# A skip product made one stage earlier, and a normaliser that reads its columns in place: an mLSTM recurrence on one core

## The chip, the cores and the metric

The kernel runs on one core of a Trainium2 chip as one program with one launch. The metric is the device time of that launch in microseconds. The kernel before took 2337.57 us (median of three executions, 2334.41 to 2339.46). One more execution was recorded by the hardware profiler; every duration below comes from that one.

A core has TensorE (PE in the profile, its weight loads PEld), VectorE (DVE), ScalarE (ACT), GpSimd (POOL) and SyncE (SP). Each takes its instructions in a fixed order; SP here issues nearly all DMA transfers. PSUM is the memory that TensorE writes to.

## The reference, cut to what matters

Two layers over 1024 latent and 256 context tokens of width 1024. Layer 0 is an attention layer, which the change doesn't touch. Layer 1 is a bidirectional mLSTM with 8 heads of 256 channels (2048 channels in all):

```
xm, z, og = split(h @ w_in, 3)                     # 2048 channels each
xc  = silu(conv5(xm))                              # over tokens
q, k, v = blockdiag(xc), blockdiag(xc), blockdiag(xm)
# per direction, per head, over chunks of tokens:
num = sqk @ v + inter * (C @ q)                    # C: the 256 x 256 state before the chunk
den = rowsum(sqk) + inter * (n . q)
h  += num / max(|den|, exp(-m))                    # both directions are added
# output
hn  = rmsnorm_per_head(sigmoid(og) * h) * head_norm
y   = ((hn + skip * xc) * silu(z)) @ w_out
```

Two places matter here. The first is `skip * xc`: a product of the convolved features, which are known before the recurrence starts, with one number per channel. The second is `max(|den|, exp(-m))`: the normaliser, for which `exp(-m)` has been worked out for all tokens, heads and directions before the recurrence.

## The kernel before, in words

All arithmetic is in 32 bits. Most matrix products are made from operands split into a high and a low part (`Ops.split`: `hi` on lines 59 to 63, `lo` on line 67) and three matmuls (`mm3`, lines 78 to 80). Layer 1 has these stages:

- **Features** (`phase_a`). A loop over 16 blocks of 128 channels. For each block TensorE projects the 1280 tokens (tile `xps`, three PSUM buffers), ScalarE copies the result to `xp` (line 962), the convolution runs on ScalarE and VectorE (lines 983 and 985), ScalarE makes `xc = silu(...)` (line 986), and SP stores `xc` to the DRAM tensor `xcT` (lines 987 and 988). Then come the gate sums (line 995), `v` (lines 1008 to 1010), `q` (tile `qt`, lines 1017 and 1018) and the gate branch `z` (two halves, line 942, stored by line 1024). The tile of `q` and the tile of `z` are two allocations of one tag, `qt`, in the pool `qp`, which has two buffers of 128x1024.
- **Gates** (`gate_scan`, inside `phase_z`). The running sums and maxima of the gates, which end in the tiles `gcol0` and `gcol1`, one for each direction: for each chunk of 128 tokens and each head four columns, of which column 1 is `exp(-m)`.
- **Recurrence** (`phase_b`). 32 units, each a head `h` and a block `c` of 256 tokens. A unit has five parts: `states` (the state updates of the next head; it loads `x` from `xcT` by line 1225 and `v` by line 1227, and transposes `x` on TensorE), `front` (multiplies `q` by `x` on TensorE, line 1257, and makes the decay factors `E`), `mid` (the numerators and denominators, tile `num` of 128 x 4 x 258, whose column 256 is the denominator), `combine` (the normaliser, the output gate, the norm) and `back` (transposes the result, adds the skip product, multiplies by `silu(z)`, stores `u`). In the code of one unit they stand in the order `mid`, `states`, `front` of the next unit, `combine`, `back` of the unit before.
- **Output projection** (`out1`).

Where the change is made: in `combine`, line 1304 copies the two columns of `exp(-m)` of each direction into a small tile `e` on POOL (two copies of 128x2), lines 1306 and 1307 make `max(|den|, e)` on VectorE and line 1308 its reciprocal, which scales `num` on ScalarE (line 1311) and VectorE (line 1312). In `back`, line 1333 multiplies the tile `x` in place by the skip factor on ScalarE (two instructions of 128x256), line 1334 adds the transposed result on VectorE, line 1335 multiplies by `sz` on POOL, and line 1338 stores `u` from the same tile. So a tile `x` is held from `states` until its store has landed, with 8 buffers.

Within these stages the instruction order of each engine's queue and of SP's is made by a planner when the program is built: it simulates the program with its own durations and takes what is ready first. (Only `phase_z` fixes an order by hand, for TensorE and ScalarE.) A changed instruction can thus shift the order around it. Buffers of a tag are handed out by the same planner.

Of the kernel before, what the change touches and what calls it, by code (L numbers as in the profile page):

```python
# [11 lines left out]
F32 = mybir.dt.float32  # L12
F32R = mybir.dt.float32r
AF = mybir.ActivationFunctionType
ALU = mybir.AluOpType
# [4 lines left out]
P = 128  # L20
D = 1024
KT = D // P
SEQ, CTX = 1024, 256
T = SEQ + CTX
NT = T // P
# [8 lines left out]
F = 2 * D  # L34
NF = F // P
MH = 8
LAT_COLS = 258
# [4 lines left out]
U = 256  # L42
# [870 lines left out]
def phase_a(nc, tc, ops, A, consts, mod, hT, S, W, graw, wx0, late):  # L913
# [3 lines left out]
    with ExitStack() as es:  # L917
        pl = lambda name, bufs=1, **kw: es.enter_context(tc.tile_pool(name=name, bufs=bufs, reuse_waits="tile", **kw))
        cp, wp, sp, qp = pl("a_c"), pl("a_w", 2), pl("a_s", 2), pl("a_q", 2)
# [2 lines left out]
        nc.sync.dma_start(wif, A["w_if"])  # L922
        cw = cp.tile([P, NF, 6], F32, name="cw")
        nc.sync.dma_start(cw, A["conv"])
        gw = [cp.tile([P, 2, P], F32R, name=f"gw{i}") for i in range(2)]
        xps = [cp.tile([P, CONV_W + 4], F32, name=f"xp{i}") for i in range(2)]
        for i in range(2):
# [3 lines left out]
        cols = [(0, 256), (LAT_COLS, 512), (LAT_COLS + 512, 512)]  # L931
# [12 lines left out]
        for f in range(NF):  # L944
# [6 lines left out]
            xp = xps[f % 2]  # L951
# [30 lines left out]
            xc = sp.tile([P, CONV_W], F32, name="xc")  # L982
# [3 lines left out]
            nc.scalar.activation(xc, xc, AF.Silu)  # L986
            nc.sync.dma_start(S["xcT"][f, :, :CTX], xc[:, :CTX])
            nc.sync.dma_start(S["xcT"][f, :, CTX:], xc[:, LAT_COLS:])
            xh = [sp.tile([P, CONV_W], F32R, name=f"xc{i}", bufs=1) for i in "hl"]
            ops.split(xh[0], xh[1], xc, "pool", "dve")  # L990

# [20 lines left out]
            qt = qp.tile([P, SEQ], F32, name="qt")  # L1012
# [62 lines left out]
def gate_scan(nc, tc, ops, A, consts, S, keep, raw, es):  # L1075
# [2 lines left out]

    cols = [keep.tile([P, NT, 4, MH], F32, name=f"gcol{d}") for d in range(2)]
    dec = keep.tile([P, 2, MH, NCH], F32, name="decay")
    pl = lambda name, bufs=1, **kw: es.enter_context(tc.tile_pool(name=name, bufs=bufs, reuse_waits="tile", **kw))
    sp, pp = pl("g_s"), pl("g_p", 1, space=PSUM)
# [17 lines left out]
    e = new("ge")  # L1102
# [48 lines left out]
    for c0 in range(0, NT, 3):  # L1151
        n = min(3, NT - c0)
# [5 lines left out]
        for d, r in enumerate(rows):  # L1158
            nc.vector.tensor_copy(cols[d][:, c0 : c0 + n], pt[:, :n, :, r.start : r.start + MH])
    nc.sync.dma_start(dec, S["dec"].rearrange("d h c -> (d h c)").unsqueeze(0).partition_broadcast(P))  # L1160
    yield cols, dec


def phase_b(nc, tc, ops, A, consts, S, W, cols, dec, hT, es_h, es_w):

    with ExitStack() as es, ExitStack() as ew, ExitStack() as eo:
        pl = lambda name, bufs=1, st=es, **kw: st.enter_context(
            tc.tile_pool(name=name, bufs=bufs, reuse_waits="tile", **kw)  # L1170
# [2 lines left out]
        cp, lp, rp, vp, xp = pl("b_c"), pl("b_l", 2), pl("b_r", 2), pl("b_v"), pl("b_x")  # L1173
# [3 lines left out]
        hns = cp.tile([P, 2, NF], F32, name="hns")  # L1177
# [11 lines left out]
        def update(h, d, i, st):  # L1189

            t, nxt = ORDERS[d][i : i + 2]
            c, a = divmod(t, 2)
            acol = cols[d][:, t, 2, h : h + 1]
            ah = [sp.tile([P, VW], F32R, name=f"ah{i}", bufs=AHB) for i in "hl"]
            va = st["v"][c][:, a]
            nc.scalar.activation(ah[0], va, AF.Copy, scale=acol)  # L1196
            nc.vector.scalar_tensor_tensor(ah[1], va, acol, ah[0].bitcast(F32), ALU.mult, ALU.subtract)  # L1197
            pk = [pc.tile([P, 512], F32, name="pc")[:, :VW] for k in range(2)]
            for k in range(2):
                ops.mm3(pk[k], [x[:, a, k * P : (k + 1) * P] for x in st["th"][c]], ah, True, True)  # L1200
            new = st["C", d, nxt] = state()
            old = st.get(("C", d, t))
            if old is None:
                for k in range(2):
                    nc.scalar.copy(new[0][:, k], pk[k])  # L1205
            else:
                decay(h, d, t, st, pk)
# [12 lines left out]
        def states(h, step, st):  # L1220

            for c in news[step]:
                hd = slice(h * 256, (h + 1) * 256)
                x = st["x"][c] = xp.tile([P, 2, U], F32, name="x", bufs=8)
                nc.sync.dma_start(x, S["xcT"][2 * h : 2 * h + 2, :, c * U : (c + 1) * U].rearrange("k p t -> p k t"))
                v = st["v"][c] = vp.tile([P, 2, VW], F32, name="v", bufs=7)
                nc.sync.dma_start(v[:, :, :256], S["v"][c * U : (c + 1) * U, hd].rearrange("(a p) d -> p a d", p=P))
                nc.gpsimd.memset(v[:, :, 256:257], 1.0)
                nc.gpsimd.memset(v[:, :, 257:258], 0.0)
                pt = pw.tile([P, 2, 2, P], F32, name="S")  # L1230
                for a in range(2):
                    for k in range(2):
                        nc.tensor.transpose(pt[:, a, k], x[:, k, a * P : (a + 1) * P], consts["idn"])
                th = st["th"][c] = [sp.tile([P, 2, 256], F32R, name=f"th{i}", bufs=THB) for i in "hl"]
                ops.split(th[0], th[1], pt.rearrange("p a k f -> p a (k f)"), "act", "dve")
            for i in (2 * step, 2 * step + 1):
                for d in range(2):
                    update(h, d, i, st)

            for d in range(2):  # L1240
                if step == 1:
                    update(h, d, NCH - 2, st)
                if step == 3:
                    t, nxt = ORDERS[d][-2:]
                    decay(h, d, t, st, st["C", d, nxt][0])
# [49 lines left out]
        def combine(h, c, st):  # L1295

            og = lp.tile([P, 2, 256], F32, name="og")
            tok = slice((c - 1) * U, c * U)
            nc.sync.dma_start(og, S["og"][tok, h * 256 : (h + 1) * 256].rearrange("(c p) d -> p c d", p=P))
            ms = rp.tile([P, 2], F32, name="ms")  # L1300
            r, e = (rp.tile([P, 2, 2], F32, name=x) for x in ("r", "e"))
            num = st["n", c]
            for d in range(2):
                nc.gpsimd.tensor_copy(e[:, d], cols[d][:, 2 * c : 2 * c + 2, 1, h])
            den = num[:, :, 256].rearrange("p (d a) -> p d a", d=2)
            nc.vector.scalar_tensor_tensor(r, den, -1.0, den, ALU.mult, ALU.max)
            nc.vector.tensor_tensor(r, r, e, ALU.max)
            nc.vector.reciprocal(r, r)
            for a in range(2):
                n0, n1 = (num[:, 2 * d + a, :256] for d in range(2))  # L1310
                nc.scalar.activation(n0, n0, AF.Copy, scale=r[:, 0, a : a + 1])
                nc.vector.scalar_tensor_tensor(n0, n1, r[:, 1, a : a + 1], n0, ALU.mult, ALU.add)
                nc.gpsimd.tensor_tensor(n0, n0, og[:, a], ALU.mult)  # L1313
                nc.scalar.activation(n1, n0, AF.Square, scale=1.0 / 16, accum_out=ms[:, a : a + 1])
            ops.rsqrt(ms, ms)
            for a in range(2):
                n0 = num[:, a, :256]
                nc.scalar.activation(n0, n0, AF.Copy, scale=ms[:, a : a + 1])

        def back(h, c, st):  # L1320

            tok = slice((c - 1) * U, c * U)
            x = st["x"][c]
            sz = xp.tile([P, 2, U], F32, name="sz", bufs=2)
            nc.sync.dma_start(sz, S["sz"][2 * h : 2 * h + 2, :, tok].rearrange("k p t -> p k t"))
            pt = pw.tile([P, 2, U], F32, name="S")
            for k in range(2):
                for a in range(2):
                    n0 = st["n", c][:, a]
                    nc.tensor.transpose(pt[:, k, a * P : (a + 1) * P], n0[:, k * P : (k + 1) * P], consts["idn"])  # L1330
            for k in range(2):
                f = 2 * h + k
                nc.scalar.activation(x[:, k], x[:, k], AF.Copy, scale=hns[:, 1, f : f + 1])
                nc.vector.scalar_tensor_tensor(x[:, k], pt[:, k], hns[:, 0, f : f + 1], x[:, k], ALU.mult, ALU.add)
            nc.gpsimd.tensor_tensor(x, x, sz, ALU.mult)  # L1335

            q = nc.gpsimd if (h, c) == units[-1][:2] else nc.sync
            q.dma_start(S["u"][2 * h : 2 * h + 2, :, tok].rearrange("k p t -> p k t"), x)
# [17 lines left out]
        for step in range(NU - 1):  # L1356
            states(0, step, sts[0])
            gate(0, ogt[step], o)
        units = [(h, c, sts[h]) for h in range(MH) for c in range(1, NU)]
        front(*units[0])  # L1360
        for i, (h, c, st) in enumerate(units):
# [12 lines left out]
            if nxt:  # L1374
                states(h + 1, c - 1, sts[h + 1])
                n = len(ogt)
# [121 lines left out]
def build(nc, tc, A, out, dbg=None):  # L1498
    ops = Ops(nc)
    with ExitStack() as es:  # L1500
        cp = es.enter_context(tc.tile_pool(name="const", bufs=1))
# [17 lines left out]
        def ahead(oT_d):  # L1519
# [3 lines left out]
        oT_d = layer0(nc, tc, ops, A, consts, mod, dp, ahead, dbg)  # L1523
        W = o0.W
        shapes = {
            "xcT": [NF, P, T], "qT": [NF, P, SEQ], "v": [T, F], "sz": [NF, P, SEQ], "og": [SEQ, F],
            "u": [NF, P, SEQ], "dec": [2, MH, NCH], "negM": [2, MH, T],
        }
        S = {n: dp.tile(s, F32, name=n + "_d") for n, s in shapes.items()}
        gk = es.enter_context(tc.tile_pool(name="gk", bufs=1))  # L1530
        with ExitStack() as el:
# [20 lines left out]
            with ExitStack() as e1:  # L1552
                scan = gate_scan(nc, tc, ops, A, consts, S, gk, graw, e1)
                next(scan)
                cols, dec = phase_z(nc, tc, ops, A, hT, S, W, range(NZ), scan)
        ew = es.enter_context(ExitStack())
        begun = phase_b(nc, tc, ops, A, consts, S, W, cols, dec, hT, eh, ew)
        out1(nc, tc, ops, A, mod, S, x1d, out, *begun)
        if dbg:
# [102 lines left out]
```

## Time and profile before

The profiled execution took 2338.38 us, of which 2336.6 us are the span from its first to its last instruction.

| engine | busy us | share of the span |
|---|---|---|
| PE | 2233.6 | 96% |
| PEld | 1957.4 | 84% |
| DVE | 1583.1 | 68% |
| ACT | 1185.5 | 51% |
| POOL | 1140.5 | 49% |

The features run from about 1050 to 1570 us of the span, the gates and the first states to about 1700 us, the 32 units of the recurrence from about 1700 to 2156 us, and the output projection takes the rest. The shares above are averages over stages with different limits. A busy time of PE includes time in which a matmul passes through the engine's pipeline, so a PE shown as busy needn't be at its peak. A line such as `ACT num L1311 <- DVE r L1308: 41.5, 24, 4.1` says that ScalarE's instruction of line 1311 waited for VectorE's of line 1308, 41.5 us in total, 24 times, at most 4.1 us. Lines 59 to 85 are helpers, which many tiles share.

### The profile page before, as it was taken

How to read it: one execution, taken by the hardware profiler on the slowest of the kernel's cores; microseconds unless marked ns; L12 is line 12 of the kernel's file. 1: busy time of each engine (PE TensorE's matmuls, PEld its weight loads, DVE VectorE, ACT ScalarE, POOL GpSimd, SP SyncE). 2: the span in 40 equal slices, each digit the busy share in tenths (PEclk: the TensorE clock that was granted, in tenths of full speed). 3: DMA queues.
4: the chain of work that ended last, by engine and by line, in shares of the span. 5: the costliest groups of instructions: out<-in, count | busy, mean ns of one | idle time of the engine just before them, and what ended most of it. 6: DMA issues, size and time to landing. Idle time of an engine off the chain costs nothing. (4 is left out here: it accounts for less than half of the span.)

```text
span 2336.6 us, 38014 instructions
## 1 busy us (share of the span) xinstructions
PE 2233.6 (96%) x13488; PEld 1957.4 (84%) x13488; DVE 1583.1 (68%) x2753; ACT 1185.5 (51%) x2864; POOL 1140.5 (49%) x1572
## 2 busy tenths in 40 slices
PE   8998999999999999998999999998999999998998
PEld 4877898998998988887878888878988888897787
DVE  5589489999998988467454443345188888898321
ACT  3512488787887877332322222233267666676211
POOL 3424356565655645462222111136557888788321
PEclk9999999999999999999999999999999999999999
DMA  7066522222311211543444333332645555545531
GB/s 262 28 197 228 160 71 79 64 68 67 89 45 58 82 54 53 191 160 123 143 131 130 120 115 109 119 122 94 193 129 164 164 168 167 163 140 169 183 126 54
DMA packets 189273, 291.10 MB, mean 125 GB/s; under 512 B 14136, under 2 KB 134712, under 8 KB 188828
## 3 DMA queue, kind: packets, MB, share of 16 engines
q1 hardware_dynamic: 188556, 286.84, 38.7%
q8 instruction: 107, 1.75, 0.3%
q0 software_dynamic: 528, 1.84, 0.2%
q14 instruction: 82, 0.67, 0.1%
HBM read 198.00 MB, written 90.62 MB: 124 GB/s over the span
## 5 line engine op out<-in xcount | busy, mean ns | idle before, releaser
L688 POOL TENSOR_SCALAR P<-P,sc 128x512 f32<-128x512 f32 (+1 forms) x384 | 243.5, 653 | 138.8 <-ACT P L644 64.8
L67 DVE TENSOR_TENSOR PTl<-tps,PTh 128x512 fp32r<-128x512 f32 x336 | 228.8, 683 | 13.5 <-ACT PTh L59 9.9
L705 PE MATMUL tps<-idn,P 128*128 128x128 f32 x1344 | 203.9, 274 | 8.7 <-POOL P L688 3.8
L63 POOL TENSOR_SCALAR wh<-raw 128x512 fp32r<-128x512 f32 (+1 forms) x96 | 91.7, 966 | 241.7 <-PE xps L79 166.6
L59 ACT CAST PTh<-tps 128x512 fp32r<-128x512 f32 x336 | 196.0, 584 | 23.4 <-PE tps L705 22.0
L644 ACT ACTIVATE P<-S,nm 128x512 f32<-128x512 f32 x256 | 177.2, 693 | 48.1 <-DVE nm L643 45.2
L643 DVE TENSOR_REDUCE nm<-S 128x1 f32<-128x512 f32 x256 | 174.9, 683 | 17.4 <-PE S L80 14.2
L67 DVE TENSOR_TENSOR wl<-raw,wh 128x1024 fp32r<-128x1024 f32 (+2 forms) x51 | 78.5, 1546 | 149.0 <-POOL wh L63 137.7
L705 PEld LDWEIGHTS tps<-idn,P 128*128 128x128 f32 x1344 | 157.8, 142 | 14.6 <-POOL P L688 4.2
L1291 PE MATMUL po<-C,q 128*128 128x258 f32 x512 | 138.8, 388 | 9.5 <-ACT num L1287 8.0
L716 PEld LDWEIGHTS po<-PTh,V 128*128 128x128 f32 x672 | 120.9, 191 | 27.7 <-ACT o L725 6.0
L716 PE MATMUL po<-PTl,V 128*128 128x256 f32 x672 | 136.7, 285 | 6.0 <-DVE PTl L67 6.0
L716 PE MATMUL po<-PTh,V 128*128 128x256 f32 x672 | 138.4, 287 | 2.5 <-ACT o L725 2.2
L78 PE MATMUL xps<-hT10h,wh 128*128 128x512 f32 (+1 forms) x384 | 139.0, 362 | 0.0
L79 PE MATMUL xps<-hT10l,wh 128*128 128x512 f32 (+1 forms) x384 | 136.9, 356 | 0.0
L80 PE MATMUL xps<-hT10h,wl 128*128 128x512 f32 (+1 forms) x384 | 136.6, 356 | 0.0
L1197 DVE SCALAR_TENSOR_TENSOR ahl<-v,gcol,ahh 128x258 fp32r<-128x258 f32 x144 | 97.0, 676 | 33.8 <-ACT ahh L1196 33.2
L985 DVE SCALAR_TENSOR_TENSOR xc<-xp,cw,xc 128x1282 f32<-128x1282 f32 x64 | 104.3, 1630 | 12.5 <-ACT xc L983 11.1
L716 PEld LDWEIGHTS po<-PTl,V 128*128 128x128 f32 x672 | 105.3, 190 | 7.5 <-DVE PTl L67 7.0
L1214 DVE SCALAR_TENSOR_TENSOR C<-C,decay,pc 128x258 f32<-128x258 f32 x224 | 101.7, 474 | 5.3 <-PE pc L80 5.3
L1291 PEld LDWEIGHTS po<-C,q 128*128 128x128 f32 x512 | 87.7, 192 | 20.3 <-ACT num L1287 11.1
L78 PE MATMUL pc<-ahh,thh 128*128 128x258 f32 x288 | 97.7, 342 | 6.1 <-ACT C L1205 2.5
(667 smaller groups left out, 7430.3 us busy)
## 6 DMA issues: line engine op xcount, KB each, us to landing
raw<-in_w_og SPq DMA_DIRECT2D x32, 512.0 KB
qT<-q_d SPq DMA_DIRECT2D x16, 960.0 KB
adaw<-in_ada_w SPq DMA_DIRECT2D x48, 256.0 KB
q_d<-qs SPq DMA_DIRECT2D x24, 512.0 KB
xt<-in_xcat SPq DMA_DIRECT2D x20, 512.0 KB
v_d<-vt SPq DMA_DIRECT2D x16, 640.0 KB
x<-xcT_d SPq DMA_DIRECT2D x40, 256.0 KB
v<-v_d SPq DMA_DIRECT2D x40, 256.0 KB
```

The costliest lines, as they stand in the source:

```text
L59: self.nc.scalar.copy(out, x)
L67: e.tensor_tensor(out, x, hi.bitcast(F32), ALU.subtract)
L78: mm(out, lh, rh, start=start, stop=False)
L79: mm(out, lh, rl, start=False, stop=False)
L80: mm(out, ll, rh, start=False, stop=stop)
L643: nc.vector.tensor_reduce(nm, S, axis=AX.X, op=ALU.max, negate=True)
L644: nc.scalar.activation(p, S, AF.Exp, bias=nm, accum_out=sm)
L688: nc.gpsimd.tensor_scalar(p, p, sc[:, a, j : j + 1], 1.0, ALU.mult, ALU.mult)
L705: nc.tensor.transpose(pt[:, kk * 256 + a * P : kk * 256 + (a + 1) * P], src, consts["idn"])
L716: nc.tensor.matmul(po, Vs[h][:, k].rearrange("p a d -> p (a d)"), PT[i][:, kk * 256 : kk * 256 + 256], start=k == 0 and i == 0, stop=k == ...
L985: nc.vector.scalar_tensor_tensor(xc, xp[:, j : j + CONV_W], cw[:, f, j : j + 1], xc, ALU.mult, ALU.add)
L1291: nc.tensor.matmul(pi[:, :VW], qa, C[:, k], start=k == 0, stop=k == 1)
```

## The change

The product `skip * xc` of the latent tokens is made in the features' stage, by one ScalarE instruction of 128x1024 for each of the 16 blocks, into a third allocation of the tag `qt`, and stored in a new DRAM tensor `xs` (512 KB for each block). `back` loads its part of `xs` (256 KB for each unit) into a tile of its own with two buffers, and adds and stores in that tile; line 1333's instructions go. The tile `x` is now last read in `front`, and has 6 buffers where it had 8. The two gate tiles become one, `both`, of which `cols[0]` and `cols[1]` are views; the normaliser reads `exp(-m)` of both directions from it by one strided operand, so line 1304's copies go, and `max(|den|, e)` is worked out as `max(max(-den, e), den)`.

```diff
@@ phase_a
+        hns = cp.tile([P, 2, NF], F32, name="hns")
+        nc.sync.dma_start(hns, A["hn_skip"])
...
             nc.sync.dma_start(S["xcT"][f, :, :CTX], xc[:, :CTX])
             nc.sync.dma_start(S["xcT"][f, :, CTX:], xc[:, LAT_COLS:])
+
+            xs = qp.tile([P, SEQ], F32, name="qt")
+            nc.scalar.activation(xs, xc[:, LAT_COLS:], AF.Copy, scale=hns[:, 1, f : f + 1])
+            nc.sync.dma_start(S["xs"][f], xs)
@@ gate_scan
-    cols = [keep.tile([P, NT, 4, MH], F32, name=f"gcol{d}") for d in range(2)]
+    both = keep.tile([P, 2, NT, 4, MH], F32, name="gcol")
+    cols = [both[:, d] for d in range(2)]
@@ phase_b, states
-                x = st["x"][c] = xp.tile([P, 2, U], F32, name="x", bufs=8)
+                x = st["x"][c] = xp.tile([P, 2, U], F32, name="x", bufs=6)
@@ phase_b, combine
-            r, e = (rp.tile([P, 2, 2], F32, name=x) for x in ("r", "e"))
+            r = rp.tile([P, 2, 2], F32, name="r")
             num = st["n", c]
-            for d in range(2):
-                nc.gpsimd.tensor_copy(e[:, d], cols[d][:, 2 * c : 2 * c + 2, 1, h])
             den = num[:, :, 256].rearrange("p (d a) -> p d a", d=2)
-            nc.vector.scalar_tensor_tensor(r, den, -1.0, den, ALU.mult, ALU.max)
-            nc.vector.tensor_tensor(r, r, e, ALU.max)
+            nc.vector.scalar_tensor_tensor(r, den, -1.0, both[:, :, 2 * c : 2 * c + 2, 1, h], ALU.mult, ALU.max)
+            nc.vector.tensor_tensor(r, r, den, ALU.max)
@@ phase_b, back
-            x = st["x"][c]
-            sz = xp.tile([P, 2, U], F32, name="sz", bufs=2)
+            x, sz = (xp.tile([P, 2, U], F32, name=n, bufs=2) for n in ("xs", "sz"))
+            nc.sync.dma_start(x, S["xs"][2 * h : 2 * h + 2, :, tok].rearrange("k p t -> p k t"))
             nc.sync.dma_start(sz, S["sz"][2 * h : 2 * h + 2, :, tok].rearrange("k p t -> p k t"))
...
-                nc.scalar.activation(x[:, k], x[:, k], AF.Copy, scale=hns[:, 1, f : f + 1])
                 nc.vector.scalar_tensor_tensor(x[:, k], pt[:, k], hns[:, 0, f : f + 1], x[:, k], ALU.mult, ALU.add)
```

## Rows read from the trace of the kernel before

**Rows 1.** Busy time by stretch (start:end, then us and count per engine): features, recurrence.
```profile
core 0: us, PE busy (x) PEld busy (x) DVE busy (x) ACT busy (x) POOL busy (x), PEclk, DMA share, GB/s
1050.00:1570.00 520.00, 508.61 (x2614) 432.89 (x2612) 246.35 (x225) 136.96 (x252) 121.55 (x114) 0.99 0.37 123
...
1700.00:2156.00 456.00, 425.63 (x2962) 390.97 (x2962) 405.53 (x820) 313.11 (x793) 358.98 (x555) 0.99 0.51 155
```

**Rows 2.** The same view, two heads of the recurrence, the shortest and the longest undisturbed.
```profile
1870.65:1927.20 56.55, 53.94 (x387) 49.96 (x386) 50.17 (x107) 39.73 (x102) 46.43 (x75) 1.00 0.55 169
...
1983.80:2041.60 57.80, 55.01 (x386) 51.08 (x385) 51.38 (x106) 40.18 (x102) 46.19 (x75) 0.97 0.53 165
```

**Rows 3.** Waits in the recurrence (us in total, times, longest us): TensorE's, then POOL's.
```profile
PE po L1291 <- ACT num L1287: 8.0, 9, 1.8
...
PE S L1257 <- DMA q<-qT_d: 3.0, 3, 1.4
...
PE pc L78 <- ACT C L1205: 2.5, 6, 1.5
PE po L78 <- POOL Eh L63: 2.3, 1, 2.3
```
```profile
POOL e L1304 <- DVE r L1307: 4.2, 10, 1.3
```

**Rows 4.** Groups by line, recurrence: busy us, mean ns | idle before.
```profile
L1333 ACT ACTIVATE x<-x,hns 128x256 f32<-128x256 f32 x64 | 29.6, 502 | 0.5 <-PE S L1257 0.2
...
L1345 ACT ACTIVATE raw<-raw 128x1024 f32<-128x1024 f32 x8 | 8.5, 1058 | 0.1
```
```profile
L1304 POOL COPY e<-gcol 128x2 f32<-128x2 f32 x64 | 17.8, 310 | 4.7 <-DVE r L1307 4.2
```
```profile
L1306 DVE SCALAR_TENSOR_TENSOR r<-num 128x4 f32<-128x4 f32 x32 | 25.5, 796 | 0.1
...
L1307 DVE TENSOR_TENSOR r<-r,e 128x4 f32<-128x4 f32 x32 | 14.6, 456 | 0.7
...
L1308 DVE RECIPROCAL r<-r 128x4 f32<-128x4 f32 x32 | 5.5, 173 | 0.6
```

**Rows 5.** Pieces of the chain that ended last (start us, us, what): first and last.
```profile
1737.37 0.40 ACT x L1333
...
2139.84 0.80 ACT x L1333 x2
```
```profile
1688.88 0.70 POOL e L1304 x4
...
2043.28 0.31 POOL e L1304 x2
```

**Rows 6.** ScalarE in order of time, one block of the features (start us, us, ...).
```profile
1434.01 1.28 ACT L986 ACTIVATE xc<-xc 128x1282 f32<-128x1282 f32 x1 [4.37 <-DVE xc L985]
1442.13 0.59 ACT L1017 COPY qt<-m 128x512 f32<-128x512 f32 x1 [6.84 <-PE m L80]
1442.61 1.09 ACT L942 ACTIVATE qt<-xps 128x512 f32<-128x512 f32 x2
```

**Rows 7.** TensorE in the same block: the first matmul of the next `xps` tile.
```profile
1443.51 0.48 PE L78 MATMUL xps<-hT10h,wh 128*128 128x512 f32 x1
```

**Rows 8.** SP's queue: a usual block's store of `xc`, then a crowded block.
```profile
1435.69 0.42 SPq L988 DMA_DIRECT2D xcT_d<-xc  x1
```
```profile
1246.12 0.42 SPq L988 DMA_DIRECT2D xcT_d<-xc  x1
1246.70 0.33 SPq L964 DMA_DIRECT2D bd<-in_bd  x1
1247.32 0.54 SPq L1010 DMA_DIRECT2D v_d<-vt  x1
```

**Rows 9.** Busy time by stretch of one us, the usual block (last two: DMA share, GB/s).
```profile
1437.00:1438.00 1.00, 1.00 (x9) 0.92 (x8) 1.00 (x1) 0.00 (x0) 0.66 (x1) 1.00 0.90 365
1438.00:1439.00 1.00, 1.00 (x11) 1.00 (x10) 0.17 (x1) 0.00 (x0) 1.00 (x1) 1.00 0.00 0
```

**Rows 10.** The chain again: waits for 512 KB loads, the first and a usual one.
```profile
1692.11 8.94 DMA raw<-in_w_og
...
1901.97 4.79 DMA raw<-in_w_og
```

**Rows 11.** SP's own waits in the recurrence (us in total, times, longest us).
```profile
SPq L1225 <- DMA u_d<-x: 50.9, 24, 3.8
```

More of the change, by code (lines that the diff above doesn't have):

```diff
@@ L1160, in gate_scan @@
     nc.sync.dma_start(dec, S["dec"].rearrange("d h c -> (d h c)").unsqueeze(0).partition_broadcast(P))
-    yield cols, dec
+    yield both, dec
 def phase_b(nc, tc, ops, A, consts, S, W, cols, dec, hT, es_h, es_w):
+    both, cols = cols, [cols[:, d] for d in range(2)]
     with ExitStack() as es, ExitStack() as ew, ExitStack() as eo:
@@ L1525, in build @@
         shapes = {
-            "xcT": [NF, P, T], "qT": [NF, P, SEQ], "v": [T, F], "sz": [NF, P, SEQ], "og": [SEQ, F],
+            "xcT": [NF, P, T], "qT": [NF, P, SEQ], "v": [T, F], "sz": [NF, P, SEQ], "xs": [NF, P, SEQ], "og": [SEQ, F],
             "u": [NF, P, SEQ], "dec": [2, MH, NCH], "negM": [2, MH, T],
```

## The prediction

> **What bounds the kernel now.** I read the busy time by stretch first, because the change touches two stages with different limits. In the features TensorE is busy 508.6 of 520 us and ScalarE only 137 [rows 1]; nothing but TensorE sets the end there, and work given to ScalarE is free as long as no matmul comes to wait for it. In the recurrence TensorE is busy 425.6 of 456 us, VectorE 405.5, POOL 359.0 and ScalarE 313.1 [rows 1]. No engine is alone at the limit: two are at nine tenths and feed each other through POOL and ScalarE. So I read next who ends TensorE's idle time: ScalarE with 8.0 + 2.5 us (it empties the PSUM tiles `po` and `pc`), a DMA with 3.0 us, POOL with 2.3 us [rows 3]; with smaller entries the idle time is 30.4 us (456 - 425.6). Then the chain of waits for pieces of exactly the instructions that go: ScalarE's line 1333 stands on it in 12 places, 7.2 us in all, POOL's line 1304 in 11 places, 5.9 us (the first and the last of each are shown) [rows 5]. An average unit takes 14.25 us (456 / 32), a head about 57 [rows 2].
>
> **The sum's base.** Durations are from the profiled execution of 2338.4 us (span 2336.6, 1.8 around it), which is 0.8 us above the median of 2337.6. I work out a difference and take it from the median.
>
> **Part 1: line 1333 goes (recurrence).** 64 instructions of 502 ns, 29.6 us started one after the other [rows 4], 0.93 us for each unit, from an engine that is busy 69% of the stage. Beside other work most of it is free. Low end: TensorE's idle time that ScalarE ends, 10.5 us [rows 3], shrinks in the proportion in which ScalarE's work does, 29.6 / 313.1 = 9.5%, which is 1.0 us. High end: all 7.2 us on the chain vanish. The ends are some 6 us apart; a piece taken off a chain pays only until the next chain is as long, and with VectorE at 89% and TensorE at 93% a next one is near. I take half, 3.6 us.
>
> **Part 2: line 1304 goes (recurrence).** 64 copies of 310 ns, 17.8 us of POOL, plus 4.2 us in which POOL stood still before them because `e` was still being read [rows 3, 4]. Low end: TensorE's 2.3 us behind POOL times 17.8 / 359.0 = 5%, 0.1 us. High end: 5.9 us on the chain and the 4.2 us of waits, 10.1 us. The copies are nearest to the chain's row; half of 5.9 is 3.0 us, and I leave the 4.2 us in the range.
>
> **Part 3: the normaliser reads `both` in place.** VectorE keeps two instructions of four elements per partition, each with two operands as before. They took 796 and 456 ns, while the reciprocal of the same size took 173 [rows 4]; the excess, (796 - 173 + 456 - 173) x 32 = 29 us, belongs to something that the one-operand instruction doesn't meet. Neither instruction loses an operand, so I count 0. Bounds: a strided operand is read from SBUF either way (0), and without the POOL copies between them a part of the excess could go. In the Trainium skill, SBUF — State Buffer, section Who interferes with whom, a VectorE instruction with two SBUF inputs contends with a GpSimd instruction that reads SBUF, and the one that comes second blocks until the other is done. The three rows above agree with it. By that rule the new pair stays exposed to POOL's long instructions just as the old one was, which speaks against a gain from reading in place; what it grants is that 64 short POOL readers fewer can block VectorE, by at most their own 17.8 us on VectorE's side. The sum by the rule would be between 0 and that; I leave it at 0, since the copies are a twentieth of POOL's time.
>
> **Part 4: the load of `xs` (recurrence).** SP issues 32 more loads of 256 KB. It adds 8.4 MB in 456 us, 18 GB/s to 155; at the present 155 GB/s for a share of 0.51 the share becomes 0.57 [rows 1]. TensorE's 3.0 us of waits for `q` [rows 3] grow in proportion by 0.4 us; I count 0.4. What is queued behind it: SP takes its issues in order, and today the load of `x` waits for the store of `u` to land 24 times, 50.9 us in all, 2.1 us each [rows 11], because store and load share the tile. After the change `x` is free as soon as `front` has read it, and the wait for a landed store passes to the load of `xs`, whose two buffers are turned over by the unit two before. So that wait is exchanged, not added, and the load has more than a unit (14 us) before line 1334 needs it. Fewer `x` buffers (6 for 8) serve a tile that lives a unit or more shorter: 0.
>
> **Part 5: the product in the features.** 16 ScalarE instructions of 128x1024. The nearest row of that size took 1058 ns [rows 4], 17 us in all. In a usual block ScalarE ends `silu` at 1435.29 and then waits 6.84 us until `qt` at 1442.13 [rows 6]; the product fits there, ends at about 1436.35, and costs nothing. Without that gap it would be 1.06 us on a stage that TensorE fills, 17 us over 16 blocks.
>
> The buffer is where I looked closer. Tag `qt` has two buffers, and now three tiles a block: product, `q`, `z`. `z`'s silu runs directly after the first half of `q` although its matmuls were done long before and ScalarE stood idle [rows 6], as if the buffers were handed out in the code's order. Then `z` takes the product's buffer and must wait until the product's store has landed. The store is issued at 1436.35, right behind the store of `xc` [rows 8]; that one's bytes are through by 1438 [rows 9]. `z` is due at 1442.61, and TensorE starts the next `xps` tile, whose PSUM buffer `z` must empty by then, at 1443.51 [rows 6, 7]: with 0.6 us for the first half (1.09 for both, overlapped) the slack behind that is 0.3 us. So the store may take 6.26 + 0.3 = 6.56 us. A 512 KB transfer took 4.79 us where nothing was in its way [rows 10], and 1.3 us for bytes queued ahead make 6.1: it fits by half a microsecond. In the crowded kind of block, where `bd` and `v` are issued right behind `xc` [rows 8], it may not; there are three of those in the trace. Low end 0; for the three at most 1.5 us each, 4.5 us; I take 1.0. The high end is a rival below. The small load of `hns` and the merged gate tile cost nothing that a row shows.
>
> **Sum.** -3.6 - 3.0 + 0 + 0.4 + 1.0 = -5.2 us, so 2337.6 - 5.2 = 2332.4 us. The ends: -7.2 - 10.1 = -17.3 us at one side, -1.1 + 0.4 + 4.5 = +3.8 at the other. The planner lays out the order anew; what that is worth is no part of the edit, and the spread of equal heads, 56.55 to 57.80 us [rows 2], is my size for it: 1.25 us a head, 10 us over eight, half of it to either side.
>
> **Rivals.**
> 1. *The freed time turns to idle.* ScalarE and POOL were not the limit; both fall idle a little longer while VectorE and TensorE run as before. For it: 89% and 93% busy. Against it: 10.5 us of TensorE's waits are for ScalarE. Gain 1.1 us, costs 1.4: 2337.9 us.
> 2. *Slower: `z` waits for the product's store.* Place: line 942 in each block, behind it on ScalarE the second half of `q` and the copy of the next `xp`, and TensorE for a `xps` buffer. It decides from a landing later than 6.56 us after the issue. A 512 KB load at a busy moment took 8.94 us [rows 10]: 2.4 us x 15 blocks = 36 us, less 6.6 in the recurrence, 2367 us; at half that overrun 18 - 6.6, 2349 us. Against it: the DMA queues are empty from 1438 to 1439 [rows 9].
> 3. *SP's queue.* The load of `xs`, waiting for a landed store, is put ahead of a load of `q` that TensorE needs soon. At 2.1 us in a quarter of the units it costs 17 us: 2348 us. For it: the wait exists today in front of `x` [rows 11]. Against it: TensorE waits for `q` only three times now [rows 3].
> 4. *The whole chain gives way.* POOL and ScalarE pace the units more than their busy shares say, and both sets of pieces and the waits go: -17.3 + 0.4, about 2321 us.
>
> **Chances.** Forecast 0.42, rival 1 0.23, rival 2 0.15, rival 3 0.07, rival 4 0.13. A difference under 0.2% (4.7 us, so 2332.9 to 2342.3) can't be told from no change. The forecast's own range is 2326 to 2336, about 0.30 of its 0.42 beyond the bound. Faster: 0.30 + 0.13 + 0.02 (rival 1, by a lucky order) = 0.45. Slower: 0.13 + 0.06 from rivals 2 and 3 and 0.03 from an unlucky order in the others, 0.22. Same: 0.33. The range reaches to rival 4 with its order's 5 us, 2316, and to rivals 2 and 3 at their middle price, 2350; beyond it lies rival 2 at full price.
>
> **What would show it.** Right: a head of 56 us or a little less; ScalarE's busy time in the recurrence near 283 us and POOL's near 341; TensorE's waits for lines 1287 and 1205 under 10 us; the features still about 520 us long with the new instruction in ScalarE's gap behind `silu`; r's two instructions still at several hundred ns. Wrong: ScalarE's line 942 with a wait for a DMA ahead of it, or a features stage that is longer (rival 2); TensorE's line 1257 waiting for `q` for much more than 3 us (rival 3); heads of 57 us with ScalarE and POOL less busy (rival 1); heads under 55.5 us (rival 4).

## The result, and the profile after

The changed kernel took 2353.20 us (median of five, 2349.05 to 2362.26) against 2337.02 us: ratio 1.0078, 95% interval 1.0061 to 1.0095. It is 16 us slower; 2332.4 was forecast, in a range of 2316 to 2350. Its profiled execution has a span of 2348.3 us.

First the busy time by stretch, as in [rows 1].

```profile
1050.00:1570.00 520.00, 507.82 (x2609) 429.54 (x2608) 242.24 (x215) 158.60 (x273) 115.22 (x109) 0.99 0.41 140
...
1700.00:2156.00 456.00, 410.75 (x2874) 380.00 (x2875) 402.26 (x804) 282.16 (x712) 330.38 (x481) 0.99 0.56 170
```

In the features TensorE is as busy as before, so no cost of the product is to be seen there. In the stretch of the recurrence ScalarE is busy 31 us less and POOL 29 us less. Not all of that was taken out: ScalarE has 81 instructions fewer there, where 64 went, and the others run later. TensorE is busy 15 us less in the same stretch: the units advance more slowly. From the first accumulation into `num` to the last (lines 1292 and 1300) the recurrence took 438.7 us before (1715.9 to 2154.6) and takes 457.9 now (1707.8 to 2165.7). That is 19 us.

The two profiled executions differ by less than that, 11.7 us of span, because layer 1 (its first matmul of `xps`) began at 1043.7 us before and at 1037.0 now. Layer 0 runs in the same order on TensorE, VectorE, ScalarE and POOL in both, and in the profiles of all the runs below its end varies between 1033 and 1044 us, so that part is no effect of the change. Counted from the first `xps`, the changed kernel takes 18.4 us more (1311.3 against 1292.9), and the recurrence accounts for it.

Next the waits of TensorE, ScalarE and SP in the recurrence, as in [rows 3, 11]; line 1213 was 1205, 1222 was 1214, 1317 was 1311, 1330 is the new load.

```profile
ACT num L1317 <- DVE r L1314: 63.2, 23, 4.7
...
PE pc L78 <- ACT C L1213: 18.0, 8, 3.2
...
PE S L1241 <- PE po L80: 6.9, 8, 1.0
PE pc L78 <- DVE C L1222: 6.0, 12, 1.3
...
PE S L1265 <- DMA q<-qT_d: 2.7, 5, 1.3
```
```profile
SPq L1330 <- DMA u_d<-xs: 60.7, 30, 4.1
```

One row of TensorE's has grown far more than the others: it waits 18.0 us, eight times, for ScalarE to empty a product `pc` into a state `C`; it was 2.5 us [rows 3]. Six of the eight waits are long, 2.5 to 3.2 us, one in each of the six middle heads. Its wait for VectorE's update of `C` has grown too, from this row of before:

```profile
PE pc L78 <- DVE C L1214: 2.3, 5, 0.7
```

The wait for `q` has not grown. Three views of the end of one head show what stands before the copy of `C`. ScalarE's queue:

```profile
1823.51 0.37 ACT L1348 COPY raw<-po 128x256 f32<-128x256 f32 x1 [1.64 <-PE po L80]
1827.41 0.91 ACT L1317 ACTIVATE num<-num,r 128x256 f32<-128x256 f32 x2 [3.54 <-DVE r L1314]
1828.34 1.28 ACT L1350 ACT_TABLE_LOAD   x1
1829.64 1.06 ACT L1350 ACTIVATE raw<-raw 128x1024 f32<-128x1024 f32 x1
1830.60 0.49 ACT L1204 ACTIVATE ahh<-v,gcol 128x258 fp32r<-128x258 f32 x1
1831.00 0.35 ACT L1213 COPY C<-pc 128x258 f32<-128x258 f32 x1
```

VectorE, for which it waits, and POOL beside it:

```profile
1824.33 0.57 DVE L1312 SCALAR_TENSOR_TENSOR r<-num,gcol 128x4 f32<-128x4 f32 x1
...
1825.94 1.23 DVE L1313 TENSOR_TENSOR r<-r,num 128x4 f32<-128x4 f32 x1
1827.20 0.18 DVE L1314 RECIPROCAL r<-r 128x4 f32<-128x4 f32 x1
```
```profile
1825.52 2.87 POOL L67 TENSOR_TENSOR wl<-raw,wh 128x512 fp32r<-128x512 f32 x2
```

And TensorE behind it:

```profile
1831.41 0.39 PE L78 MATMUL pc<-ahh,thh 128*128 128x258 f32 x1 [2.50 <-ACT C L1213]
```

ScalarE stands 3.54 us before the scaling by `r` and only then loads the table for the gate's sigmoid and runs it (2.36 us); the copy of `C` comes behind all that. Before the change the sigmoid stood ahead of the scaling in five of the six middle heads and filled a part of that wait, as here:

```profile
1889.00 1.06 ACT L1345 ACTIVATE raw<-raw 128x1024 f32<-128x1024 f32 x1
1892.02 0.91 ACT L1311 ACTIVATE num<-num,r 128x256 f32<-128x256 f32 x2 [1.96 <-DVE r L1308]
1892.83 0.63 ACT L1205 COPY C<-pc 128x258 f32<-128x258 f32 x2
```

In the changed program's queue that holds in two of the six middle heads; in the other four the scaling comes first. But the sigmoid's place is not the whole of it. In the two heads where it stands ahead (1884.07 and 2003.43 below), TensorE waits for `C` just as long:

```profile
1889.35 0.39 PE L78 MATMUL pc<-ahh,thh 128*128 128x258 f32 x1 [2.63 <-ACT C L1213]
...
2008.72 0.39 PE L78 MATMUL pc<-ahh,thh 128*128 128x258 f32 x1 [3.17 <-ACT C L1213]
```

TensorE's own queue has changed as well. Before the change it had more to do ahead of that same `pc`:

```profile
1891.00 1.03 PE L1291 MATMUL po<-C,q 128*128 128x258 f32 x4
...
1893.23 0.39 PE L78 MATMUL pc<-ahh,thh 128*128 128x258 f32 x1 [0.20 <-ACT C L1205]
```

Counted over the two traces, the `pc` that waits at 1831, 1889, 1951 and 2009 us is the same matmul as the one at 1835, 1893, 1950 and 2006 us before, and in the changed kernel three matmuls of `v` and `E` and four of `C` and `q` fewer stand ahead of it. The old order repeats itself exactly from head to head on TensorE, VectorE, ScalarE and POOL (1831 to 2060 us); the new one repeats every two heads. The sigmoids' times show it: 59.9, 54.4, 65.0, 54.4 and 62.7 us lie between them where the kernel before had 54.5 to 57.9. A part of that alternation is only the sigmoid's own place in its head; between the `pc` that waited the heads take 57.9 to 61.5 us, and 56.6 to 57.8 before.

```profile
1769.76 1.06 ACT L1350 ACTIVATE raw<-raw 128x1024 f32<-128x1024 f32 x1
...
1829.64 1.06 ACT L1350 ACTIVATE raw<-raw 128x1024 f32<-128x1024 f32 x1
...
1884.07 1.06 ACT L1350 ACTIVATE raw<-raw 128x1024 f32<-128x1024 f32 x1
...
1949.06 1.06 ACT L1350 ACTIVATE raw<-raw 128x1024 f32<-128x1024 f32 x1
...
2003.43 1.06 ACT L1350 ACTIVATE raw<-raw 128x1024 f32<-128x1024 f32 x1
...
2066.18 1.06 ACT L1350 ACTIVATE raw<-raw 128x1024 f32<-128x1024 f32 x1
```

### The profile page after: what moved, and what is told of

It is laid out like the page before. It is cut to its first block, busy times and chain, and to the rows that moved or that the text cites. A ratio compares the mean times of both kernels' runs of the same rounds, so it can differ in the third digit from the quotient of the medians.

```text
span 2348.3 us, 38034 instructions
## 1 busy us (share of the span) xinstructions
PE 2229.7 (95%) x13488; PEld 1956.7 (83%) x13488; DVE 1589.1 (68%) x2753; ACT 1179.0 (50%) x2816; POOL 1123.5 (48%) x1508
## 5 line engine op out<-in xcount | busy, mean ns | idle before, releaser
L1205 DVE SCALAR_TENSOR_TENSOR ahl<-v,gcol,ahh 128x258 fp32r<-128x258 f32 x144 | 103.6, 723 | 44.2 <-ACT ahh L1204 43.8
```

## The experiments

Three theories stood at the start: the order that the planner made anew (1), the added transfers with SP's waits (2), and a normaliser made late by reading in place (3). The first four runs undo one part each or touch one suspect.

**Only the product's part.** The normaliser as before.

```diff
...
-            nc.vector.scalar_tensor_tensor(r, den, -1.0, both[:, :, 2 * c : 2 * c + 2, 1, h], ALU.mult, ALU.max)
-            nc.vector.tensor_tensor(r, r, den, ALU.max)
+            for d in range(2):
+                nc.gpsimd.tensor_copy(e[:, d], cols[d][:, 2 * c : 2 * c + 2, 1, h])
...
+            nc.vector.scalar_tensor_tensor(r, den, -1.0, den, ALU.mult, ALU.max)
+            nc.vector.tensor_tensor(r, r, e, ALU.max)
```

> Only the product's part of the change: made in the features, stored, loaded in the recurrence, x with 6 buffers; the normaliser keeps its POOL copies and the two gate tiles. Theory 1 (order: in the changed kernel ScalarE's queue has the scaling by r ahead of the gate's sigmoid at the end of each head, waits there some 3.5 us, and TensorE waits 18 us in all for the copies of C behind it): this build has the sigmoid ahead again, so TensorE's waits for C fall from 18 to under 6 us and the time is 2333 to 2342 us. Theory 2 (the added transfers and SP's waits for the landed store of u): the traffic is all here, so it stays at 2348 to 2355 us. Theory 3 (the normaliser in place makes r late): the cause is out, so 2330 to 2338 us.

Measured: 2353.95 us, ratio 1.0077 (1.0062 to 1.0091). TensorE's waits for `C` did fall to 6.1 us, and the time did not: theory 1 in its narrow form, with the sigmoid as the one culprit, is wrong. By this run theory 2 led.

**Only the normaliser's part.** The skip product stays in the recurrence. Seen from the changed kernel:

```diff
...
-            x, sz = (xp.tile([P, 2, U], F32, name=n, bufs=2) for n in ("xs", "sz"))
-            nc.sync.dma_start(x, S["xs"][2 * h : 2 * h + 2, :, tok].rearrange("k p t -> p k t"))
+            x = st["x"][c]
+            sz = xp.tile([P, 2, U], F32, name="sz", bufs=2)
...
+                nc.scalar.activation(x[:, k], x[:, k], AF.Copy, scale=hns[:, 1, f : f + 1])
```

> Only the normaliser's part of the change: one gate tile, no POOL copies, both columns read in place; the skip product stays on ScalarE in the recurrence and x has 8 buffers. Theory 1 (order): some heads of this build have the scaling by r ahead of the sigmoid and some behind it, so TensorE waits for C in a part of the heads, 4 to 10 us, and the time is 2338 to 2347 us. Theory 2 (transfers): none were added, so 2330 to 2338 us. Theory 3 (the normaliser in place makes r late): the whole cause is here, so 2348 to 2355 us.

Measured: 2345.52 us, ratio 1.0043 (1.0030 to 1.0055). The time lies in theory 1's range, but its sign is missing: TensorE waits only 2.8 us for `C`, where 4 to 10 were expected. Each part alone is slower, by 18 and 10 us, and together they cost 16: they don't add, which speaks against a fixed price for either.

**The sigmoid first.**

```diff
-                nc.scalar.activation(n0, n0, AF.Copy, scale=r[:, 0, a : a + 1])
+                with tc.issue_after(sig[0].ins) if sig[0] else ExitStack():
+                    nc.scalar.activation(n0, n0, AF.Copy, scale=r[:, 0, a : a + 1])
...
-                nc.scalar.activation(o, o, AF.Sigmoid)
+                sig[0] = nc.scalar.activation(o, o, AF.Sigmoid)
```

> The changed kernel with one edge more for the planner: on ScalarE the scaling by r of the unit in which the gate's sigmoid is issued stands behind that sigmoid, as before the change. No data or wait is changed. Theory 1 (order): TensorE's 18 us of waits for C fall to under 6 us, heads from 58 to about 56.5 us, time 2334 to 2342 us. Theories 2 and 3 (transfers, late r): the order is no cause, so it stays within 4 us of the changed kernel, 2349 to 2357 us.

Measured: 2344.92 us, ratio 1.0042 (1.0030 to 1.0054), above theory 1's range and below that of the other two. One edge in the planner's input brings 8 us of the loss back, with the data as they were. It is not the price of the sigmoid's place alone: around that edge the planner laid out the other queues anew too (after 1600 us, of some 800 instructions of ScalarE 179 no longer follow the one that they follow in the changed kernel; of some 900 of VectorE, 271). In TensorE's waits the copies of `C` are small again, and others are larger than before the change:

```profile
PE pc L78 <- DVE C L1222: 9.3, 18, 1.4
PE S L1241 <- PE po L80: 5.3, 6, 0.9
PE S L1339 <- DVE r L1316: 3.9, 1, 3.9
PE pc L78 <- ACT C L1213: 3.5, 8, 0.9
```

**Three buffers for the loaded product.**

```diff
-                x = st["x"][c] = xp.tile([P, 2, U], F32, name="x", bufs=6)
+                x = st["x"][c] = xp.tile([P, 2, U], F32, name="x", bufs=5)
...
-            x, sz = (xp.tile([P, 2, U], F32, name=n, bufs=2) for n in ("xs", "sz"))
+            x, sz = (xp.tile([P, 2, U], F32, name=n, bufs=i) for n, i in (("xs", 3), ("sz", 2)))
```

> The changed kernel with 3 buffers for the loaded product instead of 2 (and 5 for x instead of 6, for the space), so that the load no longer waits on SP for the store of u of two units before. Theory 2 (SP's waits for the landed store, 60.7 us in the changed kernel, hold back the loads behind them): those waits fall to under 20 us and the time to 2336 to 2344 us. Theory 1 (order): the time moves with the order alone; one of two heads looked at has the sigmoid ahead in this build, the other not, so TensorE waits for C half as long, about 9 us, and the time is 2341 to 2349 us. Theory 3 (late r): unchanged, 2349 to 2357 us.

Measured: 2359.99 us, ratio 1.0108 (1.0096 to 1.0121). SP's wait for the landed store is still 57.6 us: the load only moved one unit ahead and stands behind the newest store again. So this run doesn't test that wait. Its scalings and sigmoids are in the alternating order of the changed kernel, and TensorE waits 17.8 us for `C`. The order on VectorE, ScalarE and POOL is in fact the changed kernel's throughout, and still the time is 7 us longer, with intervals that don't overlap (1.0096 to 1.0121 against 1.0061 to 1.0095). So in this order the number of buffers and the order of SP's transfers are worth something; no run here follows that up.

What was needed was a separation of data from order. The next four kernels take the finished order of one program and hold another program's recurrence in it: for each engine the instructions traced in the recurrence, less those that the other program lacks (the copies, the scalings, the loads of `xs`), are chained by edges that fix the order of issue and add no wait. In the first SP's queue is held too; in the others the planner places SP's transfers. The traces show the orders that were meant.

```diff
+    for engine, order in QUEUES.items():
+        for k, last in zip(order[1:], order):
+            dep = mybir.DependencyInfo(mybir.DependencyClass.NoSync, mybir.DependencyReason.DATA)
+            tc.add_manual_dep(todo[engine][k], todo[engine][last].name, dep, reason="queue")
```

**The normaliser's part in the old order.**

> Only the normaliser's part, with the recurrence's instructions on all five queues held in the order that they have in the kernel before (less the 64 POOL copies). Alone and freely planned this part cost 10 us. Theory 1, widened (the planner's new order is the loss, whichever edit brings it): back at 2329 to 2338 us. Theory 2 (transfers): as the kernel before here, since none are added, 2331 to 2340 us. Theory 3 (the reads in place make r late): stays at 2342 to 2348 us.

Measured: 2336.20 us, ratio 0.9993 (0.9982 to 1.0004). Its loss of 10 us is gone, and with it theory 3: this part, copies out and columns read in place, costs nothing in the old order, and gains nothing that can be told.

**The product's part in the old order.**

> Only the product's part, with the recurrence's instructions on TensorE, VectorE, ScalarE and POOL held in the order of the kernel before (less the 64 scalings on ScalarE); SP's order is left to the planner. Freely planned this part cost 18 us. Theory 1, widened (order): 2328 to 2340 us. Theory 2 (the added transfers and SP's waits): stays at 2346 to 2356 us. A mixture would lie between.

Measured: 2330.74 us, ratio 0.9974 (0.9965 to 0.9983). The transfers are all there, SP still waits 68.1 us for landed stores, and the kernel is 6 us faster than before, not 18 slower. As the cause of the loss, theory 2 falls. TensorE's waits here (line 1293 was 1287, 1211 was 1205):

```profile
PE S L1263 <- DMA q<-qT_d: 6.4, 6, 2.3
...
PE po L1297 <- ACT num L1293: 2.8, 3, 1.0
...
PE pc L78 <- ACT C L1211: 2.3, 6, 1.3
```

**The whole change in the old order.**

> The whole change, with the recurrence's instructions on TensorE, VectorE, ScalarE and POOL held in the order of the kernel before (less the copies and scalings that go); SP's order is left to the planner. Theory 1, widened (order): the loss of 17 us goes and the freed ScalarE and POOL time shows, 2326 to 2338 us. Theory 2 (transfers): 2345 to 2356 us. Theory 3 (late r): 2340 to 2348 us.

Measured: 2329.67 us, ratio 0.9975 (0.9965 to 0.9986), 7 us faster than the kernel before by the medians (2336.63 measured beside it). This build beats both kernels. Its waits:

```profile
ACT num L1317 <- DVE r L1314: 39.0, 24, 4.1
...
PE S L1265 <- DMA q<-qT_d: 5.0, 4, 1.7
...
PE pc L78 <- ACT C L1213: 2.5, 6, 1.5
PE po L1299 <- ACT num L1295: 2.2, 3, 1.0
```

The wait for `C` is back at 2.5 us and the recurrence takes 436.1 us (1711.8 to 2147.9).

**The kernel before in the new order.**

> The kernel before, nothing of the change in its data, with the recurrence's instructions on TensorE, VectorE, ScalarE and POOL held in the order of the changed kernel; its own 64 scalings, 64 copies and SP's issues are put in by the planner. Theory 1, widened (order): slow, 2347 to 2362 us, with heads of 58 us. Theories 2 and 3: the cause isn't here, so 2333 to 2342 us.

Measured: 2368.57 us, ratio 1.0140 (1.0126 to 1.0154), 32 us slower with not one byte, load or operand changed, and even above the range that theory 1 gave. The same rows as in the changed kernel:

```profile
ACT num L1311 <- DVE r L1308: 59.3, 23, 3.9
...
PE pc L78 <- ACT C L1205: 19.8, 10, 3.2
```

Its heads alternate too (60.6, 57.7, 64.4, 58.8, 64.4 us between sigmoids). It is 15 us worse than the changed kernel, which runs the same order without the 64 scalings and 64 copies: in this order the change's own work gains more than the 7 us that it gains in the old one. Which of the two parts that is, no run here shows.

The last four ask which queue carries the loss: the whole change, with one engine's queue held in the old order and the others laid out by the planner around it. The edit is that of the held builds with one entry of `QUEUES`.

> The whole change, with ScalarE's order alone held as before the change; the planner lays out the other queues around it. If ScalarE's order carries the loss of 23 us (2329.7 held, 2353.2 free): 2328 to 2338 us. If VectorE's or TensorE's does: 2342 to 2353 us, about what the sigmoid alone gave (2344.9). If holding any queue pulls the others' plan back with it: 2328 to 2338 here and also in the next two runs.

Measured: 2337.80 us, ratio 1.0014 (1.0003 to 1.0024).

> The whole change, with VectorE's order alone held. ScalarE's sigmoid then stands ahead of the scaling by r in the same heads as when ScalarE is held. If VectorE's order carries the loss, or holding any queue pulls the rest back: 2328 to 2338 us. If ScalarE's does by more than the sigmoid's place: 2340 to 2350 us.

Measured: 2333.16 us, ratio 1.0002 (0.9991 to 1.0013).

> The whole change, with TensorE's order alone held. TensorE's waits for C (18 us free) should fall here if its own order put the products pc too early behind ScalarE: 2328 to 2338 us; the same if holding any queue pulls the rest back. If the loss sits in ScalarE's or VectorE's order: 2340 to 2350 us.

Measured: 2340.06 us, ratio 1.0021 (1.0008 to 1.0033), 2 us above the one expectation and just inside the other.

> The whole change, with POOL's order alone held. Here the sigmoid's place still varies from head to head. By each theory POOL's order is not the carrier: 2342 to 2354 us. If it came to 2328 to 2338 us, POOL's order (its long two-operand instructions beside r's) would be the carrier.

Measured: 2336.28 us, ratio 1.0000 (0.9988 to 1.0011), against the expectation, which had given POOL's order no part.

Holding any one of the four leads the planner to a layout as fast as the kernel before, within 0.2%, and none alone reaches the 0.9975 of all four. So these runs don't single out a queue: with one held, the others are laid out anew. The traces tell two cases apart. With ScalarE, VectorE or TensorE held, the other queues come close to the old order: of some 800 instructions of ScalarE 0, 95 and 106 no longer follow the one that they follow in the old order, where the changed kernel has 324. With POOL held they don't: ScalarE has 271 such places, VectorE 428 of some 900 (434 in the changed kernel). That is a third layout, about as far from the old one as the slow one is, and it loses nothing. TensorE waits for `C` 3.4, 3.3, 2.2 and 3.8 us in these runs (from 1690 us on).

## Why the prediction was wrong

The step that failed is the sentence in the sum: "The planner lays out the order anew; what that is worth is no part of the edit, and the spread of equal heads, 56.55 to 57.80 us [rows 2], is my size for it: 1.25 us a head, 10 us over eight, half of it to either side." The mechanism was named and mis-sized. The runs show 2353.2 - 2329.7 = 23.5 us for it with the change's data, and 32 us with the old data, where 5 us were allowed. The spread of heads within one plan was the wrong row: the heads of [rows 2] all run the same order, instruction for instruction, so it tells nothing of what another order would do. It was also wrong to give it no direction: no row said that a fresh plan would be as good as the one at hand.

Point by point:

- **The edit's own gain** was forecast as -5.2 us and measured, in the old order, as -7.0 us (2329.67 against 2336.63). That the two are near is in part luck, since the split was off. The product's part was put at -3.6 for the scalings plus 1.4 for its costs, -2.2 us; it measured -5.9 us. The normaliser's part was put at -3.0 us and measured -0.4, inside its interval of no change. POOL's copies were on the chain in eleven places, 5.9 us, and taking them off paid nothing that can be told; ScalarE's pieces were 7.2 us. Half of the chain for both was a rule of thumb that neither followed. The low end of part 1 was off as well: with the product's part in the old order, TensorE's waits for ScalarE's lines 1287 and 1205 fell from 10.5 to 5.1 us, by half and not by a tenth. Where in the kernel the 5.9 and 7.0 us lie is not shown. The profiled executions have a recurrence of 438.1 and 436.1 us against 438.7, and from the first `xps` to the end they are 3.0 and 4.5 us shorter than before; the rest of their difference is in layer 0, which varies by itself.
- **ScalarE's busy time**, near 283 us in the stretch, was named as a sign of being right. The 282.2 us of the changed kernel match it by accident: work had moved behind 2156 us. In the old order it is 294.6 us, with the next stage's work already in the stretch.
- **Reading in place at 0** fits, though no run has it without the copies' removal. The pair took 510 and 650 ns in the changed kernel, 727 and 510 with the normaliser's part in the old order, and the reciprocal 173 in both, so it is nearly as exposed as the old pair (796 and 456 [rows 4]):

```profile
L1313 DVE TENSOR_TENSOR r<-r,num 128x4 f32<-128x4 f32 x32 | 20.8, 650 | 0.6
L1312 DVE SCALAR_TENSOR_TENSOR r<-num,gcol 128x4 f32<-128x4 f32 x32 | 16.3, 510 | 0.3
```

The Trainium skill, SBUF — State Buffer, section Who interferes with whom, states that a VectorE instruction with two SBUF inputs contends with a GpSimd instruction that reads SBUF, and that the one that comes second is blocked. The place shown above agrees: line 1313 took 1.23 us beside two POOL subtractions of 2.87 us together, and in its shortest case 150 ns.

- **The product in the features at no cost** was right as far as can be told: the stretch of `xps` takes 518 to 522 us in the runs with the product and 518 to 520 in those without. Rival 2, `z` waiting for the product's store, didn't happen: line 944 (942 before) waits for no DMA in any of the 16 blocks, and the product stands in ScalarE's gap. The prediction's margin for that store was rougher than it looked: the 4.79 us of [rows 10] was not a transfer with nothing in its way, since a load of `v` was issued 0.42 us ahead of it.

```profile
1428.55 1.27 ACT L988 ACTIVATE xc<-xc 128x1282 f32<-128x1282 f32 x1 [4.37 <-DVE xc L987]
1429.86 1.15 ACT L993 ACTIVATE qt<-xc,hns 128x1024 f32<-128x1024 f32 x1
1436.67 0.59 ACT L1023 COPY qt<-m 128x512 f32<-128x512 f32 x1 [5.66 <-PE m L80]
1437.15 1.09 ACT L944 ACTIVATE qt<-xps 128x512 f32<-128x512 f32 x2
```

- **The load of `xs`** behaved as described: SP's wait for the landed store passed to it (60.7 us, 50.9 before), and the DMA share rose to 0.56 (0.57 forecast). TensorE's wait for `q` is 2.7 us in the changed kernel, but 6.4 and 5.0 in the two held builds with the load, and 4.1 in the held build without it, so the 0.4 us counted for it may be too little. Rival 3 is out as the cause: with the same loads and waits the held builds are faster than before.
- **Rival 1**, freed time that turns to idle, fits the normaliser's part (-0.4 us) and not the product's; **rival 4** has no support. What happened, an order that loses more than the edit gains, was no rival of mine at all, only 0.03 of chance for an unlucky order, though the front of the text names the planner.

That the order on the four engines makes the loss is shown from both sides, by the change in the old order and by the kernel before in the new one. The buffers that the planner hands out along with an order were not told apart from it. What stays open is which places of the new order make up the 23 us, and why the planner preferred it. TensorE's listed waits in the recurrence and its end grew from 26.8 us in the old order to 46.6 us, 15.5 of it for `C`, about as much as the two profiled executions differ in span (19.7 us). But the wait for `C` is where this plan loses its time and not a price of the change: the product's part alone lost 18 us with 6.1 us of it.

## What to carry to other kernels

Where a planner lays out the queues, an edit has two effects, its own and that of the new plan, and the second can be several times the first: here -7 and +23 us. Tell them apart before judging an edit, by holding the old order with edges that add no wait, and by running the old kernel in the new order; a part that is slower alone and again slower with the other, without adding up, is a sign that order is at work. Holding one queue doesn't tell which queue is at fault, because the planner lays out the others anew around it. For a forecast, the spread within one plan is no measure for another plan. In this one stage, where two engines are at nine tenths, another order cost 5% of the stage with the change's data (23 us of 458) and 7% with the old data (32 us); that other stages behave so is not shown.

## What the runs showed that was not expected

A short wait on one engine became costly by order alone. In the head shown, ScalarE stood 3.54 us before a scaling that needs four numbers per partition; two VectorE instructions of four elements took 0.57 and 1.23 us of that, beside POOL, and VectorE's other work around them the rest. In the old order the scaling waits for `r` as well, in 24 places, but there the sigmoid and more of TensorE's products run meanwhile. In the new one the 2.36 us of table load and sigmoid, which waited for nothing, stood in the way of a 0.35 us copy that TensorE needed.

A queue that is itself far from its limit can steer the whole plan: holding POOL's order alone, an engine busy 72% of the stage, brought the time from 2353.2 to 2336.3 us. And a good order is not one order: that plan is a third one, about as far from the old order on ScalarE and VectorE as the slow plan is.
